# Row maxima of a sparse attention: one product of 128 rows a head, or two heads at once in products of 64 rows

## The chip, the cores and the metric

The kernel runs on one core of a Trainium2 chip. The metric is the time of one execution in microseconds (us) on the device; the median of several executions is compared. TensorE (PE in the rows) multiplies matrices, VectorE (DVE) reduces and adds, ScalarE (ACT) takes exponentials and copies, GpSimd (POOL) adds and masks, and SyncE (SP) issues most DMAs.

## The reference, cut to what matters

One layer of a decoder: a mixer of three kinds of heads, then a feed-forward block, for 1024 tokens of width 1024 in float32. The part that is changed belongs to the sparse attention with 8 query heads of 64 dimensions in two groups of four; each group shares its keys. With 1024 tokens there are 16 blocks of 64 keys, all of which are selected, so the "selected" branch is plain causal attention, and the "window" branch is causal attention over the last 512 keys.

```
s = jnp.einsum('bgrqd,bgqnld->bgrqnl', qblk, ksb)            # selected branch
p = masked_softmax(s, smask)
...
s = jnp.einsum('bgrqd,bgkd->bgrqk', qblk, kwb)               # window branch
o_win = jnp.einsum('bgrqk,bgkd->bgrqd', masked_softmax(s, wmask), vwb)
```

masked_softmax subtracts the largest score of each row before it takes the exponential, and divides by the sum. A number near the largest score serves as well, since it cancels in the division.

## The kernel before, in words

All products of full precision are made of halves: a float32 number is split into a leading half (hi) and a rest (lo) in a short format (fp32r), and hi·hi, lo·hi and hi·lo are added up in PSUM.

Stage by stage: projections and the first two mixers (to about 440 us of the profiled execution), the sparse attention together with the output projection (about 440 to 790 us), the feed-forward block (the rest). In the sparse attention the 1024 queries are swept in 8 blocks of 128, from the last (7) to the first (0). For each block there are two passes over the scores.

- The maxima (`ns_max`, lines L1012 to L1062). For each branch and each head, QS (128 partitions: 64 rows of leading halves of the queries, then 64 rows of rests) is the stationary matrix, and KH (the leading halves of the keys, held twice, in partitions 0 to 63 and 64 to 127) streams past it, up to 512 keys at a time: a product of 128 rows that sums hi·hi and lo·hi (L1037, tiles `nsms` and `nsmw`). A group of nb heads shares a bank of PSUM (one head of 512 or 384 keys, two of 256, four of 128). Where a causal or window edge lies in it, a small bf16 product with the identity adds the mask (L1044). VectorE then takes the negated maximum of each row (L1047, `ns_nm`). When all are done, they are transposed and written by DMA into two rows of M2 (L1061).
- The scores and values (`ns_attn`). The scores are made again with the maxima inside the product (L1077 with M2, L1078 with QS), exponentiated (L1079), and multiplied with the values in products of 64 columns, two at a time (L1097, tiles `nsos`, `nsow`). L1127 sums denominators in products of 32 columns.

The mixer before it has products of 64 rows as well: L513 (tile `mla`) multiplies heads in turn on partitions 0 to 63 and 64 to 127, into two banks, behind products of 32 rows (L510).

The order on each engine is set when the program is built. `merge` interleaves lists of tasks by stated costs: the maxima of the next block beside the scores of the present one, and the output projection (L929, `wo`) as filler. A scheduler then moves single instructions within what data and banks allow. The banks for the maxima (`mx`) are three for block 7 and two for the others: `set_banks(st=(0, 1), ot=(2,), ch=(3,), mt=(7,), rw=(3,), mx=(4, 5), d=(6, 7))`.

`ns_q` loads the queries of a block by three DMAs of 256 KB: hi into QS[0:64], lo into QS[64:128], hi into M2[0:64].

Of the kernel before, what the change touches and what calls it, by code (L numbers as in the profile page):

```python
# [12 lines left out]
ALU = mybir.AluOpType  # L13
AX = mybir.AxisListType
PSUM = bass.MemoryType.PSUM

P = 128
# [14 lines left out]
def f32(ap):  # L32
    return ap.bitcast(F32)
# [3 lines left out]
def kernel(  # L37
# [20 lines left out]
    nc = tc.nc  # L58
# [22 lines left out]
    def unit(name, shape=(P, 1024), dt=F32):  # L81
        v = up.tile([P, UW], dt, tag="u", name=name)[:, 0:math.prod(shape[1:])]
        return v.rearrange("p (a b) -> p a b", a=shape[1]) if len(shape) == 3 else v
# [4 lines left out]
    def bank(name, shape=(P, 512), tag="d"):  # L88
        ids = groups[tag]
        turns[tag] = turns.get(tag, -1) + 1  # L90
        i = ids[turns[tag] % len(ids)]
        return mm.tile(list(shape), F32, tag=f"p{i}", name=name, bufs=1)
# [29 lines left out]
    def small(name, n, dt=F32, p=P, bufs=None):  # L122
        return sm.tile([p, n], dt, tag=name, name=name, bufs=bufs)
# [13 lines left out]
    identb = const.tile([P, P], BF16, name="identb")  # L137
# [191 lines left out]
    def run(tasks):  # L329
        for _, fn in tasks:  # L330
            fn()
# [103 lines left out]
    cols = mlp.tile([P, 3, NT, 4], F32, name="cols", bufs=1)  # L435
# [195 lines left out]
    KH, KL = {}, {}  # L631
# [319 lines left out]
    def ntile(name, shape, tag):  # L951
        pool, bufs = (wkp[0], 3) if tag == "pt" else (wkn, {"acc": 4, "hc": 3, "ot": 2, "y": 3}[tag])
        return pool.tile(shape, F32, tag=tag, name=name, bufs=bufs)
# [3 lines left out]
    CB, CN = "w", 1  # L957
    ns_st = [dict() for _ in range(NT)]

    def ns_q(qt):  # L960
        st = ns_st[qt]
        st["y"] = ntile(f"yns{qt}", [P, 512], "y")
        QS = unit(f"QS{qt}", (P, 8, P), F32R)
        M2 = unit(f"M2{qt}", (P, 8, P), F32R)
        for dst, z in ((QS[0:64], 0), (QS[64:128], 1), (M2[0:64], 0)):
            src = nq_d[z, 0, :, qt * P:(qt + 1) * P]
            nc.sync.dma_start(f32(dst), bass.AP(tensor=src.tensor, offset=src.offset,
                                                ap=[[S, 64], [64 * S, 8], [1, P]]))
        st["QS"], st["M2"] = QS, M2
        st["nm"] = small("ns_nm", 16, bufs=3)  # L970
        st["nm2"] = small("ns_nm2", 16, bufs=3)
        st["cf"] = small("ns_cf", 24, bufs=4)

    def ns_cmp_score(qt, i):
        st = ns_st[qt]
        if i == 0:
            st["c"] = bank(f"nsc{qt}", tag="ch")
            nc.tensor.matmul(st["c"].rearrange("p (h c) -> p h c", h=8), identb,
                             mcmp[:, qt, None, :].to_broadcast([P, 8, 64]), start=True, stop=False)
        h, z = i // 2, i % 2  # L980
        nc.tensor.matmul(st["c"][:, h * 64:(h + 1) * 64], st["QS"][:, h, :], (kcs_h, kcs_l)[z][:, h // 4, :],
                         start=False, stop=(i == 15))

    def ns_cmp(qt):
        st = ns_st[qt]
        gt = gns[:, qt, :].rearrange("p (h b) -> p h b", b=3)
        sps = st["c"]
        nmc = small("nmc", 8)
        nc.vector.tensor_reduce(nmc, sps.rearrange("p (h c) -> p h c", h=8), axis=AX.X, op=ALU.max, negate=True)
        nc.vector.tensor_scalar(nmc, nmc, 1e29, None, op0=ALU.min)  # L990
        pc = ntile(f"pc{qt}", [P, 8, 64], "hc")
        dn = small("nsd", 8, bufs=2)
        for h in range(8):
            nc.scalar.activation(pc[:, h, :], sps[:, h * 64:(h + 1) * 64], AF.Exp, bias=nmc[:, h:h + 1],
                                 accum_out=dn[:, h:h + 1])
        nc.vector.tensor_scalar(dn, dn, 1e-30, None, op0=ALU.max)
        nc.vector.reciprocal(dn, dn)
        nc.vector.tensor_tensor(dn, dn, gt[:, :, 0], op=ALU.mult)
        nc.vector.tensor_tensor(pc, pc, dn[:, :, None].to_broadcast([P, 8, 64]), op=ALU.mult)
        pt = bank(f"nscT{qt}", tag="ch")  # L1000
        for j in range(4):
            nc.tensor.transpose(pt[:, j * P:(j + 1) * P], pc[:, 2 * j:2 * j + 2, :].rearrange("p a c -> p (a c)"), ident)
        pcT = ntile(f"pcT{qt}", [P, 4, P], "hc")
        nc.scalar.copy(pcT.rearrange("p j q -> p (j q)"), pt)
        py = bank(f"nscy{qt}", tag="ch")
        for j in range(4):
            nc.tensor.matmul(py[:, j * P:(j + 1) * P], pcT[:, j, :], vcs[:, j // 2].rearrange("p a d -> p (a d)"),
                             start=True, stop=True)
        nc.scalar.copy(st["y"], py)

    def ns_range(br, qt):
        k0 = 0 if br == "s" else max(0, qt - 4)  # L1012
        return k0, qt + 1 - k0

    def ns_max(qt):
        st = ns_st[qt]
        tasks = []
        cs = [(0.1, lambda i=i: ns_cmp_score(qt, i)) for i in range(16)]
        for bi, br in enumerate(("s", "w")):
            k0, nk = ns_range(br, qt)  # L1020
            kl = nk * P
            for pi, off in enumerate(range(0, kl, 512)):
                w = min(512, kl - off)
                nb = 512 // w

                def piece(h0, bi=bi, br=br, pi=pi, off=off, w=w, nb=nb, k0=k0, kl=kl):
                    hs = range(h0, min(8, h0 + nb))
                    mx_ = bank(f"nsm{br}{qt}_{off}_{h0}", tag="mx")
                    n = len(hs)
                    m3 = mx_[:, 0:n * w].rearrange("p (h k) -> p h k", h=n)  # L1030
                    mk = []
                    if br == "w" and qt >= 4 and off == 0:
                        mk.append((0, mtail))
                    if off + w == kl:
                        mk.append((w - P, mdiag))
                    for i, h in enumerate(hs):
                        nc.tensor.matmul(m3[:, i, :], st["QS"][:, h, :], KH[br, h // 4][:, k0 * P + off:k0 * P + off + w],  # L1037
                                         start=(i == 0), stop=(i == n - 1 and not mk))
                        if br == CB:
                            for _ in range(CN if w >= 256 else 0):  # L1040
                                if cs:
                                    cs.pop(0)[1]()
                    for z, (c0, m) in enumerate(mk):
                        nc.tensor.matmul(m3[:, :, c0:c0 + P], identb, m[:, None, :].to_broadcast([P, n, P]),  # L1044
                                         start=False, stop=(z == len(mk) - 1))
                    dst = (st["nm"] if pi == 0 else st["nm2"])[:, 8 * bi + h0:8 * bi + h0 + n]
                    nc.vector.tensor_reduce(dst, m3, axis=AX.X,  # L1047
                                            op=ALU.max, negate=True)
                    if pi == 1 and h0 + n >= 8:
                        a = st["nm"][:, 8 * bi:8 * bi + 8]  # L1050
                        nc.vector.tensor_tensor(a, a, st["nm2"][:, 8 * bi:8 * bi + 8], op=ALU.min)
                for h0 in range(0, 8, nb):
                    tasks.append((0.42 * w * min(nb, 8) / 1000.0 + 0.05, lambda h0=h0, f=piece: f(h0)))

        def rows():
            pt = bank(f"nsr{qt}", tag="rw")
            nc.tensor.transpose(pt[0:16, 0:P], st["nm"], ident)
            mr = small("ns_mr", P, F32R, 16, bufs=1)
            nc.vector.tensor_copy(mr, pt[0:16, 0:P])
            for bi in range(2):  # L1060
                nc.sync.dma_start(f32(st["M2"][64 + bi:65 + bi, :, :]), f32(mr[8 * bi:8 * bi + 8, :]))  # L1061
        tasks.append((0.15, rows))  # L1062
        return [(0.05, lambda: ns_q(qt))] + tasks + [(CC + 0.05, lambda: (run(cs), ns_cmp(qt)))]

    def ns_attn(qt):
# [83 lines left out]
    T0 = (0,)  # L1149
    set_banks(d=(0,), ch=(0,), mt=(0,), rw=(4,), ds=(2, 3), mx=(4, 5, 1), dt=(6,), po=(7,))  # L1150
    merge((da[-CUT:], 1.0), (wo_loads(0) + merged((ns_max(ORDER[0]), 1.0), (wo_tasks(0, T0), 1.0)), 1.0))
    qstk.close()
    wkp.append(nstk.enter_context(tc.tile_pool(name="wkp", bufs=3, side="right")))
# [197 lines left out]
    w = ff_first  # L1351
    for c in range(NP):
# [5 lines left out]
        if c + 1 < NP:  # L1358
            w = []
# [186 lines left out]
```

## Time and profile before

| | |
|---|---|
| median of 3 runs | 1459.52 us (1459.01 to 1461.6) |
| the profiled execution | 1457.8 us, its span 1456.1 us |
| TensorE busy | 1408.1 us (97% of the span) |
| VectorE, ScalarE, GpSimd busy | 983.0, 661.1, 315.9 us |
| mean granted TensorE clock | 0.991 |

The span goes from the first to the last instruction of the profiled execution. [...]

### The profile page before, as it was taken

The page shows a single profiled execution, that of the slowest core. Times are in us where ns is not written, and L with a number is a line of the kernel's source. Part 1 is how long each engine was busy: PE and PEld are TensorE (multiplying, and loading weights), DVE is VectorE, ACT ScalarE, POOL GpSimd, SP SyncE. Part 2 cuts the span into 40 slices and gives each one's busy share as a digit, 9 for nine tenths or more (in the row PEclk, how much of TensorE's full clock was granted, in tenths as well). Part 3 has the DMA queues.
Part 4 walks back from the last instruction along what each step waited for, and adds up shares of the span by engine and source line. Part 5 has one row for each costly group of instructions (what it writes and reads, how often), then busy time and mean ns, then how long its engine had stood idle before and what let it go on. Part 6 is the DMA issues. An engine that isn't in the chain of part 4 may idle for free.

```text
span 1456.1 us, 19441 instructions
## 1 busy us (share of the span) xinstructions
PE 1408.1 (97%) x7031; PEld 1066.8 (73%) x7031; DVE 983.0 (68%) x1756; ACT 661.1 (45%) x1309; POOL 315.9 (22%) x358
## 2 busy tenths in 40 slices
PE   8999999899989999999999999999999999999997
PEld 7998777666756555556666887888888788788875
DVE  6313588788778665766545968777776877985366
ACT  6414333687572433334444545555544543443243
POOL 2000033222241343443333111111111004200051
PEclk9999999999988999999999999999999999999999
DMA  6301222111255011012312327444435896796522
GB/s 214 102 1 30 69 89 93 52 33 37 80 133 121 30 37 44 15 37 73 95 52 73 109 87 233 154 147 139 146 137 214 294 407 216 278 357 191 174 88 115
DMA packets 107551, 181.77 MB, mean 125 GB/s; under 512 B 11552, under 2 KB 66368, under 8 KB 107456
## 3 DMA queue, kind: packets, MB, share of 16 engines
q1 hardware_dynamic: 96704, 144.89, 31.1%
q0 software_dynamic: 10752, 35.66, 6.4%
q8 instruction: 55, 0.90, 0.3%
q14 instruction: 40, 0.33, 0.1%
HBM read 134.31 MB, written 46.14 MB: 124 GB/s over the span
## 4 chain that ended last, share of the span: by engine, by line
PE 78%; DVE 9%; ACT 4%; issue 3%; POOL 2%; DMA 2%; DVEq 0%; SPq 0%; POOLq 0%; ACTq 0%
PE ff L1417 17%; PE ff L1320 15%; PE wo L929 6%; PE ff L1252 4%; PE pml_p L324 3%; PE nsos L1097 2%; PE nq_p L324 2%; PE pD_p L244 2%; PE pB_p L244 2%; PE dao L871 2%; PE pC_p L244 2%; PE nsow L1097 2%; PE pA_p L244 1%; POOL x2b L1435 1%; PE nsms L1037 1%
## 5 line engine op out<-in xcount | busy, mean ns | idle before, releaser
L1320 PE MATMUL ff<-h2h,fw 128*128 128x512 f32 x312 | 97.5, 393 | 1.0 <-ACT fw L126 0.7
L1226 POOL DMA_DIRECT2D act_d<-fn x52 | 28.1, 540 | 206.2 <-ACT fn L1334 151.6
L1320 PEld LDWEIGHTS ff<-h2h,fw 128*128 128x128 f32 x312 | 58.6, 188 | 15.0 <-ACT fw L126 1.2
L1079 ACT ACTIVATE nsps<-nsts 128x512 f32<-128x512 f32 x72 | 40.1, 596 | 64.1 <-PE nsts L1078 44.7
L1327 DVE TENSOR_TENSOR fn<-fn,ff 128x512 f32<-128x512 f32 x65 | 43.5, 686 | 35.9 <-PE ff L1320 35.9
L835 DVE TENSOR_REDUCE da_nm<-das 128x1 f32<-128x512 f32 (+3 forms) x96 | 51.5, 551 | 18.6 <-PE das L832 16.0
L126 ACT ACTIVATE fw<-fs 128x512 fp32r<-128x512 f32 x52 | 32.6, 632 | 66.5 <-PE ff L1320 65.1
L1320 PE MATMUL ff<-h2l,fw 128*128 128x512 f32 x156 | 61.1, 392 | 0.0
L1047 DVE TENSOR_REDUCE ns_nm<-nsms 128x1 f32<-128x512 f32 (+3 forms) x76 | 48.5, 656 | 18.5 <-PE nsms L1044 9.2
L841 ACT ACTIVATE dap<-das,da_nm 128x512 f32<-128x512 f32 (+3 forms) x96 | 55.1, 584 | 12.7 <-DVE da_nm L838 6.8
L1435 POOL TENSOR_TENSOR x2b<-x2b,tmq 128x512 f32<-128x512 f32 x12 | 22.0, 1871 | 152.6 <-ACT tmq L1454 152.6
L1417 PE MATMUL ff<-b0h,a0h 128*128 128x512 f32 x128 | 50.4, 395 | 2.5 <-ACT fn L1333 2.5
L1079 ACT ACTIVATE nspw<-nstw 128x512 f32<-128x512 f32 x60 | 33.3, 604 | 39.1 <-PE nstw L1078 26.4
L1417 PE MATMUL ff<-b1l,a1h 128*128 128x512 f32 x128 | 50.5, 394 | 0.5 <-DVE b1l L128 0.5
L1417 PE MATMUL ff<-b0h,a0l 128*128 128x512 f32 x128 | 50.6, 395 | 0.0
L1417 PE MATMUL ff<-b2h,a2l 128*128 128x512 f32 x128 | 50.4, 394 | 0.0
L1417 PE MATMUL ff<-b1h,a1h 128*128 128x512 f32 x128 | 50.3, 393 | 0.0
L1417 PE MATMUL ff<-b1h,a1l 128*128 128x512 f32 x128 | 50.3, 393 | 0.0
L1417 PE MATMUL ff<-b2h,a2h 128*128 128x512 f32 x128 | 50.3, 393 | 0.0
L1417 PE MATMUL ff<-b2l,a2h 128*128 128x512 f32 x128 | 50.2, 392 | 0.0
L1417 PE MATMUL ff<-b0l,a0h 128*128 128x512 f32 x128 | 50.1, 392 | 0.0
L931 DVE TENSOR_TENSOR x<-x,wo 128x512 f32<-128x512 f32 x32 | 22.0, 686 | 40.2 <-PE wo L929 40.2
(548 smaller groups left out, 4313.2 us busy)
## 6 DMA issues: line engine op xcount, KB each, us to landing
ar<-act_d SPq DMA_DIRECT2D x48, 512.0 KB
f1r<-in_w_ff_dram SPq DMA_DIRECT2D x32, 512.0 KB
wr<-in_w_ff_dram SPq DMA_DIRECT2D x32, 512.0 KB
act_d<-fn POOLq DMA_DIRECT2D x52, 256.0 KB, 2.6
x<-in_x_dram SPq DMA_DIRECT2D x16, 512.0 KB
act_d<-as POOLq DMA_DIRECT2D x16, 512.0 KB, 3.3
wo<-in_w_ff_dram SPq DMA_DIRECT2D x16, 512.0 KB
wr<-in_w_ff_dram SPq DMA_DIRECT2D x32, 256.0 KB
```

The lines of the kernel that those rows point to most:

```text
L244: nc.tensor.matmul(pt[:, :NA], T_stat(a, kt, t), b[kt // 4][:, kt % 4, :], start=(i == 0), stop=(i == 23))
L324: nc.tensor.matmul(pt, a[:, kt, :], T_mov(b, kt, h), start=(i == 0), stop=(i == 23))
L835: nc.vector.tensor_reduce(nm[:, z:z + 1], b[:, 0:n1 - n0], axis=AX.X, op=ALU.max, negate=True)
L841: nc.scalar.activation(p_[:, n0:n1], b[:, 0:n1 - n0], AF.Exp, bias=nm[:, 0:1], accum_out=dens[:, 2 * z + m:2 * z + m + 1])
L929: nc.tensor.matmul(po, m_[a][:, k, :], wo[4 * part + k][b][:, ns_], start=(i == 0), stop=(i == 11))
L1047: nc.vector.tensor_reduce(dst, m3, axis=AX.X, op=ALU.max, negate=True)
L1079: nc.scalar.activation(pT[:, g, :], s_, AF.Exp)
L1097: nc.tensor.matmul(st["o", br][64 * g:64 * g + 64, :], vsw[kt // 4][:, kt % 4, c0:c0 + 64], pT[:, g, :], start=(k == 0), stop=(k == nk - 1))
L1252: nc.tensor.matmul(pt, a, T_mov(b, kt, h), start=(i == 0), stop=(i == 23))
L1320: nc.tensor.matmul(pt, w[:, x_, kt, :], b[y_][kt // 2][:, kt % 2, :], start=(i == 0), stop=(i == 11))
L1327: nc.vector.tensor_tensor(dst, s_, pt, op=ALU.add)
L1417: nc.tensor.matmul(banks[4 * p + t], a[y][:, 512 * p + t * P:512 * p + t * P + P], b[x_][:, 512 * p:512 * p + 512], start=first and i == 0 ...
```

## The change

The row maxima are taken of hi·hi alone; lo·hi is left out of them (the scores themselves are made as before). A product of a head then needs 64 rows. Two heads, or two groups of nb heads, form a pair: one on partitions 0 to 63 (QS[0:64] with KH[0:64]) into one bank, the other on partitions 64 to 127 (M2[64:128], into which a fourth DMA now loads the hi queries, with KH[64:128]) into the next bank. The mask products of both banks stand behind the pair's products, and the two reductions behind these.

```
-        for dst, z in ((QS[0:64], 0), (QS[64:128], 1), (M2[0:64], 0)):
+        for dst, z in ((QS[0:64], 0), (QS[64:128], 1), (M2[64:128], 0), (M2[0:64], 0)):
...
-                    mx_ = bank(f"nsm{br}{qt}_{off}_{h0}", tag="mx")
-                    m3 = mx_[:, 0:n * w].rearrange("p (h k) -> p h k", h=n)
...
-                    for i, h in enumerate(hs):
-                        nc.tensor.matmul(m3[:, i, :], st["QS"][:, h, :], KH[br, h // 4][:, k0 * P + off:k0 * P + off + w],
-                                         start=(i == 0), stop=(i == n - 1 and not mk))
+                    mx_ = [bank(f"nsm{br}{qt}_{off}_{h}", tag="mx")[:, 0:n * w].rearrange("p (h k) -> p h k", h=n)
+                           for h in (h0, h0 + n)]
+                    for i in range(n):
+                        for u, (rs, T) in enumerate(((slice(0, 64), "QS"), (slice(64, 128), "M2"))):
+                            h = h0 + n * u + i
+                            nc.tensor.matmul(mx_[u][:, i, :], st[T][rs, h, :], KH[br, h // 4][rs, cols],
+                                             start=(i == 0), stop=(i == n - 1 and not mk))
                         if br == CB:
-                            for _ in range(CN if w >= 256 else 0):
+                            for _ in range(2 * CN if w >= 256 else 0):
                                 if cs:
                                     cs.pop(0)[1]()
-                    for z, (c0, m) in enumerate(mk):
-                        nc.tensor.matmul(m3[:, :, c0:c0 + P], identb, m[:, None, :].to_broadcast([P, n, P]),
-                                         start=False, stop=(z == len(mk) - 1))
-                    dst = (st["nm"] if pi == 0 else st["nm2"])[:, 8 * bi + h0:8 * bi + h0 + n]
-                    nc.vector.tensor_reduce(dst, m3, axis=AX.X,
-                                            op=ALU.max, negate=True)
+                    for u in range(2):
+                        for z, (c0, m) in enumerate(mk):
+                            nc.tensor.matmul(mx_[u][:, :, c0:c0 + P], identb, m[:, None, :].to_broadcast([P, n, P]),
+                                             start=False, stop=(z == len(mk) - 1))
+                    for u in range(2):
+                        h = h0 + n * u
+                        dst = (st["nm"] if pi == 0 else st["nm2"])[:, 8 * bi + h:8 * bi + h + n]
+                        nc.vector.tensor_reduce(dst, mx_[u], axis=AX.X, op=ALU.max, negate=True)
...
-                for h0 in range(0, 8, nb):
-                    tasks.append((0.42 * w * min(nb, 8) / 1000.0 + 0.05, lambda h0=h0, f=piece: f(h0)))
+                for h0 in range(0, 8, 2 * nb):
+                    tasks.append((0.84 * w * nb / 1000.0 + 0.1, lambda h0=h0, f=piece: f(h0)))
```

The scheduler makes a new order of this. On TensorE, at the window maxima of block 7 (heads 2, 3, 4; `nsmw_0_2` is head 2, `mtail` the mask of the window's edge), there stood before:

```order
L1037 MATMUL nsmw_0_2_4875<-KHw_4404,QS_4648 128x512
L1044 LDWEIGHTS identb
L1044 MATMUL nsmw_0_2_4875<-mtail,identb 128x128
L1037 MATMUL nsmw_0_3_4880<-KHw_4404,QS_4648 128x512
L1044 LDWEIGHTS identb
L1044 MATMUL nsmw_0_3_4880<-mtail,identb 128x128
```

and now, where QS is the lower and M the upper half of the rows:

```order
L871 MATMUL dao_7_4832<-daPT_7_0_1_4845,dav_930 64x128
L1040 MATMUL nsmw_0_2_4876<-KHw_4404,QS_4648 128x512
L1040 MATMUL nsmw_0_3_4877<-KHw_4404,M_4649 128x512
L1048 LDWEIGHTS identb
L1048 MATMUL nsmw_0_2_4876<-mtail,identb 128x128
L1048 LDWEIGHTS identb
L1048 MATMUL nsmw_0_3_4877<-mtail,identb 128x128
L863 MATMUL daT_7_4_0_4906<-ident,dap_7_4620 128x128 x3
```

Here the two heads of a pair stand side by side, and so do their masks. At the first maxima of block 6, on the same engine, there stood before:

```order
L1037 MATMUL nsms_0_3_5044<-KHs_4204,QS_5015 128x512
L1037 MATMUL nsms_0_0_5023<-KHs_4204,QS_5015 128x512
L1037 MATMUL nsms_0_5_5065<-KHs_4207,QS_5015 128x512
L929 MATMUL wo_1_0_5223<-woh_4578,mTh_1_5219 128x512
L1037 MATMUL nsms_0_2_5038<-KHs_4204,QS_5015 128x512
L1037 MATMUL nsms_0_7_5080<-KHs_4207,QS_5015 128x512
```

and now:

```order
L1040 MATMUL nsms_0_1_5026<-KHs_4204,M_5017 128x512
L916 MATMUL mT_1_5221<-ident,mix_1_5219 128x128
L1062 MATMUL nsr_4943<-ident,ns_nm 16x128
L916 MATMUL mT_1_5221<-ident,mix_1_5219 128x128 x3
L1040 MATMUL nsms_0_0_5025<-KHs_4204,QS_5016 128x512
L929 MATMUL wo_1_0_5230<-woh_4578,mTh_1_5226 128x512
L1040 MATMUL nsms_0_3_5041<-KHs_4204,M_5017 128x512
L1002 MATMUL nscT_4974<-ident,pc_4960 128x128 x4
L1040 MATMUL nsms_0_2_5040<-KHs_4204,QS_5016 128x512
```

Here the scheduler has set products of 128 rows between the heads of a pair, since the second head's bank comes free later than the first's.

## Rows read from the trace of the kernel before

**Rows 1.** The page's first row: busy time of each engine, its share, instructions

```profile
PE 1408.1 (97%) x7031; PEld 1066.8 (73%) x7031; DVE 983.0 (68%) x1756; ACT 661.1 (45%) x1309; POOL 315.9 (22%) x358
```

**Rows 2.** Busy time of each engine by stretch, then granted clock, DMA share, GB/s

```profile
443.00:467.00 24.00, 23.40 (x159) 16.55 (x158) 21.75 (x43) 4.11 (x10) 2.18 (x4) 1.00 0.44 98
467.00:500.00 33.00, 29.78 (x105) 14.95 (x107) 25.54 (x45) 16.78 (x53) 11.20 (x10) 0.84 0.20 58
500.00:755.00 255.00, 250.07 (x1241) 153.10 (x1239) 155.91 (x245) 100.16 (x237) 97.88 (x76) 1.00 0.16 49
```

**Rows 3.** TensorE's waits from 435 to 760 us: us in total, times, longest

```profile
PE nsms L1037 <- DVE ns_nm L1047: 3.1, 4, 1.7
...
PE nsmw L1037 <- DVE ns_nm L1047: 0.4, 1, 0.4
```

**Rows 4.** Groups by line and shape: count, busy us, mean ns, idle before

```profile
L1037 PE MATMUL nsms<-KHs,QS 128*128 128x512 f32 x48 | 21.5, 490 | 1.7 <-DVE ns_nm L1047 1.5
L1037 PE MATMUL nsmw<-KHw,QS 128*128 128x512 f32 x40 | 17.8, 453 | 0.4 <-DVE ns_nm L1047 0.4
...
L1047 DVE TENSOR_REDUCE ns_nm<-nsms 128x1 f32<-128x512 f32 x48 | 32.1, 684 | 10.9 <-PE nsms L1037 8.8 <-PE nsms L1044 1.8
```

**Rows 5.** TensorE in order of time: start, length, line, rows*columns, x count

```profile
247.84 0.39 PE L324 MATMUL nq_p<-hTl,nq_hi 128*128 128x512 f32 x1
248.16 0.49 PE L510 MATMUL mla<-cmD,selr 32*128 32x256 f32 x2
248.58 0.71 PE L513 MATMUL mla<-mlqk,mlqk 64*128 64x128 f32 x8
249.23 0.50 PE L324 MATMUL daq_p<-hTh,daq_hi 128*128 128x512 f32 x1
249.56 0.39 PE L324 MATMUL daq_p<-hTh,daq_lo 128*128 128x512 f32 x1
249.79 0.39 PE L324 MATMUL daq_p<-hTl,daq_hi 128*128 128x512 f32 x1
```

**Rows 6.** The same view of 248.57 to 248.60 us alone

```profile
248.58 0.38 PE L513 MATMUL mla<-mlqk,mlqk 64*128 64x128 f32 x2
```

**Rows 7.** The same view around a visit of products of 64 columns

```profile
662.67 0.39 PE L1078 MATMUL nstw<-QS,KHw 128*128 128x512 f32 x1
662.99 1.08 PE L1097 MATMUL nsow<-nspw,vsw 128*64 128x512 f32 x4
664.00 0.50 PE L1077 MATMUL nstw<-M,KLw 66*128 66x512 f32 x1
664.33 0.40 PE L1078 MATMUL nstw<-QS,KHw 128*128 128x512 f32 x1
```

**Rows 8.** The same view: products of 64 and of 256 columns streamed

```profile
451.92 0.28 PE L981 MATMUL nsc<-kcs_h,QS 128*128 128x64 f32 x1
452.03 0.28 PE L981 MATMUL nsc<-kcs_l,QS 128*128 128x64 f32 x1
...
534.87 0.40 PE L1037 MATMUL nsms<-KHs,QS 128*128 128x256 f32 x2
535.11 0.28 PE L1044 MATMUL nsms<-mdiag,identb 128*128 128x256 bf16 x1
```

**Rows 9.** The same view: heads with a mask, and two masks in a row

```profile
490.28 0.28 PE L1044 MATMUL nsms<-mdiag,identb 128*128 128x128 bf16 x2
490.50 1.08 PE L1097 MATMUL nsos<-nsps,vsw 128*64 128x512 f32 x4
...
622.89 0.47 PE L1037 MATMUL nsms<-KHs,QS 128*128 128x512 f32 x1
623.21 0.23 PE L1044 MATMUL nsms<-mdiag,identb 128*128 128x128 bf16 x1
623.25 0.48 PE L1037 MATMUL nsms<-KHs,QS 128*128 128x512 f32 x1
```

**Rows 10.** The DMA queue's issues that write M2 from the stored queries

```profile
M<-nq_d SPq DMA_DIRECT2D x8, 256.0 KB
```

More of the change, by code (lines that the diff above doesn't have):

```diff
@@ L1026, in piece @@
                 def piece(h0, bi=bi, br=br, pi=pi, off=off, w=w, nb=nb, k0=k0, kl=kl):
-                    hs = range(h0, min(8, h0 + nb))
-                    mx_ = bank(f"nsm{br}{qt}_{off}_{h0}", tag="mx")
-                    n = len(hs)
-                    m3 = mx_[:, 0:n * w].rearrange("p (h k) -> p h k", h=n)
+                    n = nb
+                    cols = slice(k0 * P + off, k0 * P + off + w)
                     mk = []
@@ L1046, in piece @@
-                    dst = (st["nm"] if pi == 0 else st["nm2"])[:, 8 * bi + h0:8 * bi + h0 + n]
-                    nc.vector.tensor_reduce(dst, m3, axis=AX.X,
-                                            op=ALU.max, negate=True)
-                    if pi == 1 and h0 + n >= 8:
+                    for u in range(2):
+                        for z, (c0, m) in enumerate(mk):
+                            nc.tensor.matmul(mx_[u][:, :, c0:c0 + P], identb, m[:, None, :].to_broadcast([P, n, P]),
+                                             start=False, stop=(z == len(mk) - 1))
@@ L1050, in piece @@
+                    for u in range(2):
+                        h = h0 + n * u
+                        dst = (st["nm"] if pi == 0 else st["nm2"])[:, 8 * bi + h:8 * bi + h + n]
+                        nc.vector.tensor_reduce(dst, mx_[u], axis=AX.X, op=ALU.max, negate=True)
+                    if pi == 1 and h0 + 2 * n >= 8:
                         a = st["nm"][:, 8 * bi:8 * bi + 8]
                         nc.vector.tensor_tensor(a, a, st["nm2"][:, 8 * bi:8 * bi + 8], op=ALU.min)
-                for h0 in range(0, 8, nb):
-                    tasks.append((0.42 * w * min(nb, 8) / 1000.0 + 0.05, lambda h0=h0, f=piece: f(h0)))
+                for h0 in range(0, 8, 2 * nb):
+                    tasks.append((0.84 * w * nb / 1000.0 + 0.1, lambda h0=h0, f=piece: f(h0)))
```

## The prediction, made before the changed kernel ran

> **What bounds the kernel now.** The page's first row: TensorE is busy 97% of the span, no other engine over 68% [rows 1]. Averages mix stages, so next the busy time by stretch, over the time in which the maxima are made: TensorE is busy 23.4 of 24, 29.8 of 33 and 250.1 of 255 us, VectorE 155.9 of the last 255 [rows 2]. From 443 to 755 us TensorE therefore sets the pace, with 312 − 303.25 = 8.8 us of idle time. Third, what it waits for there: for the products of the maxima 3.5 us in all, each time for VectorE's reduction to free a bank [rows 3]. So a microsecond that TensorE saves or loses there counts almost fully, and what VectorE does counts only through banks.
>
> Fourth, what a product costs. Its record of 0.39 us is not its price: in order of time, products of 512 columns start 0.23 us apart [rows 5]. Those of 256 take 0.24 / 2 = 0.12, and those of 64 or 128 columns 0.11, where the load of the weights sets the pace [rows 8]; for 384 I scale 0.23 to 0.17.
>
> **What is removed: the second head of a pair.** There are 192 head products: 88 of 512 columns [rows 4], 24 of 384, 24 of 256 and 56 of 128, counted in the order. Two heads side by side on different halves of the rows should cost one: in the mixer before, the products of 64 rows do so, since two start within 0.03 us of each other [rows 6]. That row shows it for 128 columns; for 512 no row does.
>
> But a pair saves only where its heads stand side by side. In the order of the changed kernel that holds for 23 pairs of 512, 6 of 384, 8 of 256 and 24 of 128; 42 of the 88 heads of 512, about half, stand alone. The saving: 23 × 0.23 + 6 × 0.17 + 8 × 0.12 + 24 × 0.11 = 5.3 + 1.0 + 1.0 + 2.6 = **9.9 us**.
>
> **What is added: steps in and out of products of 64 rows.** The view in order of time shows what a visit to another shape of the array costs. From 247.84 to 249.56 us TensorE goes from full products to 32 rows, to 64 rows and back, in 1.72 us [rows 5]. Plain prices for the same work: 0.23 + 2 × 0.12 + 4 pairs × 0.11 + 0.23 = 1.14. The 0.58 over that falls on three steps, **0.19 us a step**. One half of it shows as the late start of the next product (0.32 for 0.23 going in), the other as a slow first product (0.33 for 0.23 coming out). The visit to 64 columns has the same two signs, 0.32 and 0.33 [rows 7]: after a step the weights are not loaded behind the product that runs, but in the open. Beside a narrow product, where the load sets the pace anyway, I charge only one half, 0.10; that is an estimate from these two rows.
>
> The order has 96 visits to 64 rows. Into them: 31 from wide products (0.19 each, 5.9 us), 36 from narrow ones or masks (0.10, 3.6 us), and 29 straight from a visit to 64 or 32 columns, where the step out of that was paid before (0). Out of them: 13 to wide products (2.5 us), 23 to narrow ones (2.3), 3 to column visits (0.3), and 57 to a mask. The last cost nothing new: a full product followed by a bf16 mask already starts the mask 0.32 after itself instead of 0.23 [rows 9]. Sum **+14.6 us** for 106 paid steps, 0.14 on average.
>
> **What is moved: the masks.** Their number stays (105, now 106), but in the order they stand in 70 groups where there were 104. A head with its mask takes 0.36 us, 0.13 over a bare one [rows 9]. The second of two masks still has to run. Where two stand in a row, the visit to 64 columns behind them starts 0.22 after the first; less the 0.09 of a late start that is 0.06 a mask [rows 9]. So each group less saves 0.07, with 0.13 as the upper bound (the second mask free) and 0.05 as the lower: 34 × 0.07 = **−2.4 us**.
>
> **What is only covered.** VectorE makes the same reductions at 0.68 us [rows 4], off the path that sets the end. SP issues 8 more loads of 256 KB, a fourth beside three for each block [rows 10], ahead of M2's lower half and of the loads for the output projection behind it on the queue. The DMA engines are at 0.16 to 0.44 there [rows 2], and the order issues the loads of a block before the scores of the block before it, so I cost them at nothing; without that cover the upper head, and the scores and `wo` products queued behind it on TensorE, wait for one more load a block. The pair now wants both banks of `mx`. The scheduler has answered with the separated heads, which is charged above; what it leaves of waiting I set equal to the 3.5 us of now, with nothing and twice that as bounds.
>
> **The sum.** +14.6 − 9.9 − 2.4 = **+2.3 us**. On the profiled execution that is 1457.8 + 2.3 = 1460.1; the median of the runs lies 1.7 above that execution, so 1459.5 + 2.3 = **1461.8 us**. A measurement of this kernel can tell about 0.2%, which is 2.9 us.
>
> The row on two products of 64 rows shows that a pair costs one head while TensorE stays in that shape [rows 6], and the row on the visit that getting there costs 0.19 a step [rows 5]. The Trainium skill, TensorEngine Tiling (Array Packing), section Theoretical Speedup, puts the factor at up to 2 for a contraction of 64 or less; its section Key Properties warns that a change of tiling mode drains TensorE. By the factor alone the sum would be the −16.7 us that stands under "all of it" below; by the rows it is the +2.3 above. The trace agrees with the warning.
>
> **The rivals.**
>
> *Dearer: the pairs do not overlap at 512 columns, or every step costs the full 0.19.* For it: rows 6 are of 128 columns, where the load of the weights hides what two streams into two banks do. Against it: nothing in the trace. No saving on the 23 wide pairs makes +2.3 + 5.3 = +7.6 us; all 106 steps at 0.19 make 20.1 − 9.9 − 2.4 = +7.8. Either gives about **1467**, both 1473.
>
> *New waits.* A pair needs two free banks and one more load; behind the waiting product stand the scores that ScalarE needs. If the waits of rows 3 double and a block's start slips by 0.2 us eight times, it is +2.3 + 3.5 + 1.6 = +7.4 at worst, **1465** in the middle. Against it: VectorE has 35% of its time free.
>
> *Faster: cheap steps.* Here the change ends on the other side. If every one of the 106 steps costs only the late start, 0.10, they make 10.6, and with 0.13 for each mask group saved (4.4) the sum is −3.7: **1455.8**. It decides at a mean of 0.12 a step. For it: many steps lie beside other steps or masks, where both halves may merge. Against it: the 0.58 of rows 5 lies beside such steps too, and is not merged. The idle time of 467 to 500 us, where the clock stands at 0.84 [rows 2], could also shrink by the new order, by a similar 3 to 4 us.
>
> *All of it.* Every pair overlaps and no step costs anything: half of 88 × 0.23 + 24 × 0.17 + 24 × 0.12 + 56 × 0.11 = 33.4, so −16.7 us, **1442.8**. The order speaks against it, as half of the wide heads stand alone.
>
> **How the numbers follow.** Nearly balanced, within 2.9 us: 0.40. Dearer 0.20 and new waits 0.15, both slower: 0.35. Cheap steps or a luckier order 0.22 and all of it 0.03, both faster: 0.25. The predicted time is the balanced 1461.8. The range goes up over the single dearer cases, not to both at once, and down past the cheap steps, 1455 to 1469; it leaves out "all of it" and the ends of the dearer cases, not quite 2 in 10. The likeliest case's own range is 1456.6 to 1462.4.
>
> **What would show it.** In the changed trace, order of time: a pair of 512 columns starts within 0.03 us and the next product 0.4 us later (overlap right) or 0.6 (wrong). A full product before a lone head starts it 0.32 later, and the one after the head is slow by 0.1: steps right. TensorE's busy time between 443 and 760 us up by about 2.3 us, with the stage as much longer. Waits of the head products for `ns_nm` near 3.5 us, none for the loads of M2. Wrong would be: a stage shorter by over 3 us (steps cheaper than charged), or longer by over 5 with pairs that start one after the other (no overlap), or with idle time on `ns_nm` (banks). Any difference after 800 us, where the feed-forward block runs as before, would not be from this sum.

## The result and the profile after

| kernel | median of its runs | ratio to before, 95% interval |
|---|---|---|
| before | 1459.3 us (6 runs, 1457.8 to 1462.8) | |
| changed | 1476.7 us (6 runs, 1470.3 to 1495.6) | 1.0120 [1.0086, 1.0154] |

The change makes the kernel 1.2% slower: 17.4 us by the medians, 15.4 by the two profiled executions (spans 1471.5 and 1456.1 us). That is beyond the predicted range of 1455 to 1469. The changed kernel also scatters more, and its time goes with the granted clock: 1470.3 us at a mean of 0.983, 1478.0 at 0.976, 1492.0 at 0.967. (The longest run, and the profiled run of experiment 4 below, are slow ones, over 1.5% above the fastest of the same kernel: the ratios leave them out, and no trace of them is read here.)

First the page's row of busy time, beside [rows 1]:

```profile
PE 1431.6 (97%) x7031; PEld 1068.7 (73%) x7031; DVE 983.2 (67%) x1756; ACT 661.0 (45%) x1309; POOL 318.1 (22%) x358
```

TensorE still sets the pace, and is busy 23.5 us longer with as many instructions. Next the busy time by stretch, as in [rows 2] (PE, PEld, DVE, ACT, POOL, granted clock, DMA share, GB/s):

```profile
443.00:467.00 24.00, 23.43 (x99) 15.13 (x100) 16.39 (x33) 2.69 (x7) 2.18 (x4) 0.78 0.58 110
467.00:500.00 33.00, 32.71 (x130) 19.01 (x127) 18.03 (x34) 12.30 (x46) 5.93 (x7) 0.66 0.32 84
500.00:755.00 255.00, 252.62 (x1202) 139.06 (x1201) 159.46 (x252) 103.23 (x241) 97.39 (x75) 1.00 0.18 49
```

The last stretch keeps its clock of 1.00. In the first two the granted clock is 0.78 and 0.66, where it was 1.00 and 0.84, and in the first TensorE gets through 99 products where it made 159. Third, slices of 5 us inside these, of the changed kernel:

```profile
455.00:460.00 5.00, 5.00 (x27) 3.15 (x25) 3.24 (x5) 0.00 (x0) 0.00 (x0) 0.99 0.05 11
460.00:465.00 5.00, 5.00 (x24) 3.29 (x23) 3.51 (x9) 0.43 (x1) 0.72 (x1) 0.69 0.00 0
465.00:470.00 5.00, 5.00 (x27) 3.38 (x26) 1.39 (x3) 0.16 (x1) 1.46 (x3) 0.50 0.06 16
470.00:475.00 5.00, 5.00 (x18) 2.91 (x17) 2.66 (x4) 0.87 (x2) 0.00 (x0) 0.50 0.00 0
```

TensorE is recorded busy without a gap, before the clock falls and after, and yet it goes to 0.50, the lower of its two levels, 1.2 GHz. So it isn't idle time that came in. The view of its waits says the same, beside the 3.5 us of [rows 3]:

```profile
PE nsms L1040 <- DVE ns_nm L1053: 0.8, 3, 0.3
...
PE nsmw L1040 <- DVE ns_nm L1053: 0.3, 1, 0.3
```

Waits for banks fell from 3.5 to 1.1 us. Last, how long the stage is. For each kernel, the view of the heads' products (duration in ns as least, median and most; then the first and the last start) gives the time from the first head of the selected branch to the last of the window branch; before, then changed:

```profile
L1037 PE MATMUL nsms<-KHs,QS x96: 221/397/796, 443.8 to 738.6; 128*128 128x512 f32 x48, 128*128 128x384 f32 x16, 128*128 128x256 f32 x16, 128*128 128x128 f32 x16
L1037 PE MATMUL nsmw<-KHw,QS x96: 221/352/505, 456.9 to 742.9; 128*128 128x512 f32 x40, 128*128 128x128 f32 x40, 128*128 128x384 f32 x8, 128*128 128x256 f32 x8
```

```profile
L1040 PE MATMUL nsms<-KHs,QS x48: 269/440/792, 445.2 to 752.7; 64*128 64x512 f32 x24, 64*128 64x384 f32 x8, 64*128 64x256 f32 x8, 64*128 64x128 f32 x8
...
L1040 PE MATMUL nsmw<-KHw,M x48: 268/435/793, 465.0 to 758.1; 64*128 64x512 f32 x20, 64*128 64x128 f32 x20, 64*128 64x384 f32 x4, 64*128 64x256 f32 x4
```

From 443.8 to 742.9 is 299.1 us, from 445.2 to 758.1 is 312.9: the stage of the maxima is 13.8 us longer. It begins 1.4 us later, and 0.2 of the 15.4 are left for all that follows.

### The profile page after: what moved, and what is told of

It is laid out like the page before. It is cut to its first block, busy times and chain, and to the rows that moved or that the text cites. A ratio compares the mean times of both kernels' runs of the same rounds, so it can differ in the third digit from the quotient of the medians.

```text
span 1471.5 us, 19461 instructions
## 1 busy us (share of the span) xinstructions
PE 1431.6 (97%) x7031; PEld 1068.7 (73%) x7031; DVE 983.2 (67%) x1756; ACT 661.0 (45%) x1309; POOL 318.1 (22%) x358
## 4 chain that ended last, share of the span: by engine, by line
PE 82%; DVE 8%; ACT 3%; POOL 2%; issue 2%; DMA 2%; DVEq 0%; POOLq 0%; SPq 0%; ACTq 0%
PE ff L1422 17%; PE ff L1325 16%; PE wo L929 6%; PE ff L1257 4%; PE pml_p L324 3%; PE nq_p L324 2%; PE nsos L1102 2%; PE dao L871 2%; PE pD_p L244 2%; PE pB_p L244 2%; PE pC_p L244 2%; PE nsms L1040 2%; PE nsow L1102 2%; PE nsmw L1040 1%; PE pA_p L244 1%
## 5 line engine op out<-in xcount | busy, mean ns | idle before, releaser
L1053 DVE TENSOR_REDUCE ns_nm<-nsmw 128x1 f32<-128x512 f32 (+3 forms) x62 | 39.4, 667 | 22.5 <-PE nsmw L1048 22.1
```

The source lines that it names most:

```text
L1053: nc.vector.tensor_reduce(dst, mx_[u], axis=AX.X, op=ALU.max, negate=True)
```

## The experiments

Two measures serve for all of them. **Stage** is the time just read, from the first to the last head product. **Time at the lower level** is worked out from the granted clock c of 447 to 515 us, in which blocks 7 and 6 have their maxima: 68 us × 2 × (1 − c). The rows of before and of the changed kernel, in this order:

```profile
447.00:515.00 68.00, 64.20 (x310) 38.42 (x309) 52.12 (x94) 23.45 (x66) 18.54 (x19) 0.92 0.19 47
```

```profile
447.00:515.00 68.00, 67.04 (x267) 38.09 (x265) 44.44 (x84) 22.24 (x65) 15.11 (x16) 0.77 0.29 69
```

That is 10.9 us for before and 31.3 for the changed kernel. Three theories stood against each other: the clock (A), waits and the new order (B), and the price of the steps between shapes (C). All experiments compare medians of 4 to 12 runs with runs of the kernel before on the same chip: one chip for 1 to 4, one for 5 to 8, one for 9, where before takes 1460.9, 1460.0 and 1460.0 us. (The 29 us at half clock that two expectations give for before are of its whole execution.)

**1. The new order with products of 128 rows.** Order, banks, grouped masks and the fourth load of the changed kernel stay; each head takes all of QS and KH, so lo·hi is in the maxima again.

```
-    nc.tensor.matmul(mx_[u][:, i, :], st[T][rs, h, :], KH[br, h // 4][rs, cols], ...
+    nc.tensor.matmul(mx_[u][:, i, :], st["QS"][:, h, :], KH[br, h // 4][:, cols], ...
```

> The changed kernel with the same pairs, banks, loads and the same order of instructions, but each head's product again has all 128 rows (QS with the whole of KH), so no step to another shape of the array is left. It computes hi.hi + lo.hi as before the change. Theory A (the clock: the visits to 64 rows let the granted clock fall to 1.2 GHz between 460 and 490 us): time at half clock back near the 29 us of before, time 1457 to 1462. Theory B (order, banks, fourth load: new waits): it keeps the loss, 1470 to 1476. Theory C (direct price of the steps, no clock): 1457 to 1462 too, and the clock of the changed kernel would have been an accident.

Measured: 1450.5 us, ratio 0.9930 [0.9918, 0.9942], the fastest kernel of this study, and 6.5 us under the least that any theory expected. On TensorE its order is that of the changed kernel but for a few products ahead of the first maxima. Its windows of blocks 7 and 6:

```profile
447.00:515.00 68.00, 65.89 (x348) 40.03 (x347) 56.24 (x102) 27.47 (x74) 20.41 (x20) 1.00 0.28 68
...
470.00:475.00 5.00, 3.86 (x18) 2.44 (x19) 5.00 (x17) 2.02 (x8) 2.34 (x4) 1.00 0.06 14
```

No time at the lower level, though TensorE sits idle for 1.14 of the 5 us from 470 on. And the view of its heads' products:

```profile
L1040 PE MATMUL nsms<-KHs,QS x96: 274/394/584, 446.4 to 732.1; 128*128 128x512 f32 x48, 128*128 128x384 f32 x16, 128*128 128x256 f32 x16, 128*128 128x128 f32 x16
L1040 PE MATMUL nsmw<-KHw,QS x96: 229/337/505, 459.5 to 737.1; 128*128 128x512 f32 x40, 128*128 128x128 f32 x40, 128*128 128x384 f32 x8, 128*128 128x256 f32 x8
```

The stage is 290.7 us, 8.4 under before. So the order and the load cost nothing, they gain, and B falls. The 64-row shape alone costs 312.9 − 290.7 = 22.2 us.

**2. Products of 66 rows in the order of before.** 66 rows are taken to be no smaller shape of the array (L1077 has them too, [rows 7]; the lag below bears it out), so there are no steps and no pairs; of lo·hi two rows of 64 stay in the maxima.

```
-    nc.tensor.matmul(m3[:, i, :], st["QS"][:, h, :], KH[br, h // 4][:, ...], ...
+    nc.tensor.matmul(m3[:, i, :], st["QS"][0:66, h, :], KH[br, h // 4][0:66, ...], ...
```

> The kernel before, with one edit: each head's product takes the first 66 of the 128 rows (all leading halves, two rows of the rests; the remaining 62 rows of the rests are left out of the maxima). 66 rows need no step to another shape. Theory A1 (half the rows in use is what lets the clock fall): more time at half clock than the 29 us of before in 440 to 500 us, 1463 to 1473. Theory A2 (the steps in and out are what lets it fall): as before, 1457 to 1462. Theories B and C: as before, 1457 to 1462.

Measured: 1471.9 us, ratio 1.0074 [1.0060, 1.0087]. Nothing but the rows in use was changed, and TensorE gets the same products in the same order as before. The windows:

```profile
447.00:515.00 68.00, 65.03 (x259) 38.86 (x259) 47.28 (x85) 21.56 (x62) 16.04 (x17) 0.72 0.18 45
...
455.00:460.00 5.00, 5.00 (x29) 3.90 (x29) 4.29 (x11) 0.00 (x1) 0.51 (x1) 0.72 0.02 3
460.00:465.00 5.00, 5.00 (x25) 3.36 (x26) 1.14 (x2) 0.58 (x1) 1.68 (x4) 0.50 0.16 25
```

The clock is down here too with TensorE busy all the time. The heads' products:

```profile
L1037 PE MATMUL nsms<-KHs,QS x96: 225/402/797, 444.4 to 750.0; 66*128 66x512 f32 x48, 66*128 66x384 f32 x16, 66*128 66x256 f32 x16, 66*128 66x128 f32 x16
L1037 PE MATMUL nsmw<-KHw,QS x96: 222/396/796, 457.7 to 754.2; 66*128 66x512 f32 x40, 66*128 66x128 f32 x40, 66*128 66x384 f32 x8, 66*128 66x256 f32 x8
```

38.1 us at the lower level, 27.2 more than before, and a stage of 309.8 us, 10.7 longer. As the order is the same, one product can be sought in both traces. The head at 500.54 us of before is the one at 511.69 here:

```profile
500.54 0.50 PE L1037 MATMUL nsmw<-KHw,QS 128*128 128x512 f32 x1
```

```profile
511.69 0.55 PE L1037 MATMUL nsmw<-KHw,QS 66*128 66x512 f32 x1
```

The lag is 0.6 us at the first head, 11.15 here, where the last time at the lower level ends, and 11.3 at the last head, 242 us later. So the whole loss falls into the time in which the clocks differ, and at a clock of 1.00 66 rows cost what 128 do. A is confirmed without any step. It also gives a rate: 10.7 / 27.2 = 0.39 us lost for each us at 1.2 GHz (an estimate, from rounded clocks).

**3 and 4. The change in blocks 5 to 0 alone, and in blocks 7 and 6 alone.** Each has the pairs and masks of the changed kernel in its blocks, and the code of before in the others (`if qt <= 5`, `if qt > 5`); the fourth load stands in all blocks of both.

> The change in blocks 5 to 0 alone; blocks 7 and 6 have the products of 128 rows. Theory A: the stretch up to 500 us keeps its clock, and what is left is the direct price of the steps in the other blocks, 0 to +3 us: 1458 to 1464. Theory B: waits come with every block, about three quarters of the loss: 1468 to 1472. Theory C: three quarters of the loss as well, 1468 to 1472.

> The change in blocks 7 and 6 alone; the others have the products of 128 rows. Theory A: nearly the whole loss, with 55 to 70 us at half clock, 1468 to 1476. Theory B and theory C: a quarter of the loss, 1462 to 1465.

Measured: 1458.1 us, ratio 0.9982 [0.9972, 0.9992], for blocks 5 to 0; 1479.8 us, ratio 1.0123 [1.0106, 1.0139], for blocks 7 and 6, more than the 1468 to 1476 expected. The loss of the changed kernel comes with blocks 7 and 6, where its clock falls. But the 0.2% for blocks 5 to 0 is no gain of these blocks. In that kernel blocks 7 and 6 have the products of before, with the fourth load and in another order, and there the clock holds:

```profile
447.00:515.00 68.00, 65.26 (x343) 39.53 (x341) 56.02 (x101) 26.95 (x73) 20.24 (x20) 1.00 0.32 71
```

Here are two products up to which it and the kernel before have done the same work on TensorE; of before, then of the kernel with the change in blocks 5 to 0:

```profile
503.36 0.39 PE L929 MATMUL wo<-wol,mTh 128*128 128x512 f32 x1
...
717.62 1.08 PE L1097 MATMUL nsos<-nsps,vsw 128*64 128x512 f32 x4
```

```profile
498.76 0.39 PE L929 MATMUL wo<-wol,mTh 128*128 128x512 f32 x1
...
718.42 1.08 PE L1133 MATMUL nsos<-nsps,vsw 128*64 128x512 f32 x4
```

(L1133 is L1097 of before.) It is 4.6 us ahead at the first and 0.8 behind at the second. So the change costs about 5 us in the later blocks, at a clock of 1.00. The first two gain some 6 without it, as the first head started 1.9 us later than before (445.7 for 443.8).

**5. The kernel of experiment 1 without the fourth load.**

```
-        for dst, z in ((QS[0:64], 0), (QS[64:128], 1), (M2[64:128], 0), (M2[0:64], 0)):
+        for dst, z in ((QS[0:64], 0), (QS[64:128], 1), (M2[0:64], 0)):
```

> The order of the changed kernel (two heads to a task, masks of both behind them) with products of 128 rows, and without the fourth load of a block. Two banks and one load more were the price that the theory of new waits named. If the load cost something, this ends below the 1450.5 us of the same kernel with the load, by 1 us or more; if it is hidden, as the prediction held, it ends at 1450.5 within 2 us. Granted clock 1.00 between 467 and 755 us either way.

Measured: 1454.9 us, ratio 0.9957 [0.9941, 0.9973]. Less work, and 4.4 us slower, which neither theory expected. Without the load the scheduler makes another order in blocks 7 and 6, and the lower level comes back for a few us:

```profile
447.00:515.00 68.00, 65.08 (x336) 39.79 (x334) 56.25 (x102) 25.40 (x70) 19.13 (x19) 0.97 0.20 54
```

In 68 × 2 × 0.03 = 4.1 us at the lower level, at the rate of experiment 2 about 1.6 us are lost, and the stage, from 448.1 to 740.9 us, is 2.1 longer than in experiment 1. The rest of the 4.4 falls outside the stage and is not explained. That the load itself is hidden is not contradicted, but not shown by itself either.

**6. 64 rows in blocks 5 to 0, 128 rows in blocks 7 and 6, in the order of experiment 1.** This prices the steps and the pairs at a clock of 1.00. The edit, against experiment 1:

```
+    R = slice(0, P) if qt >= 6 else rs
-    nc.tensor.matmul(mx_[u][:, i, :], st["QS"][:, h, :], KH[br, h // 4][:, cols], ...
+    nc.tensor.matmul(mx_[u][:, i, :], st[T if qt < 6 else "QS"][R, h, :], KH[br, h // 4][R, cols], ...
```

> As the kernel with 128 rows in the new order (1450.5 us), but the maxima of blocks 5 to 0 in products of 64 rows, and only those. The prediction's own prices for these six blocks: 68 paid steps +9.2, 45 pairs -7.5, so +1.8 us; with 0.10 for each of the 27 exits into a mask, which it charged at nothing, +4.5. Theory that the clock carries most of the loss: the clock stays at 1.00 in 500 to 755 us, and the time is 1452 to 1455. Theory that each step costs far more than charged (the 22.8 us of the changed kernel over the one with 128 rows, spread over all 96 visits): two thirds of it, about 1465.

Measured: 1456.9 us, ratio 0.9977 [0.9966, 0.9989]; 6.4 us over experiment 1 by the medians, which is above the range expected of the theory of the clock and far from the 1465 of dear steps. The window of blocks 7 and 6:

```profile
447.00:515.00 68.00, 65.86 (x342) 39.69 (x342) 53.98 (x97) 27.26 (x73) 21.04 (x21) 1.00 0.28 66
```

The clock holds. The first and the last group of the heads' products:

```profile
L1041 PE MATMUL nsms<-KHs,QS x64: 270/440/580, 444.0 to 734.4; 128*128 128x512 f32 x24, 64*128 64x512 f32 x12, 128*128 128x384 f32 x8, 64*128 64x256 f32 x8
...
L1041 PE MATMUL nsmw<-KHw,M x32: 270/410/502, 532.5 to 739.8; 64*128 64x512 f32 x12, 64*128 64x128 f32 x12, 64*128 64x384 f32 x4, 64*128 64x256 f32 x4
```

The stage is 295.8 us, 5.1 longer than in experiment 1. The prediction's prices give +1.8; with 0.10 for the 27 exits into a mask, +4.5. The rest of the shape's 22.2 us, 17.1, is lost by blocks 7 and 6.

**7. 128 rows, of which 64 hold zeros.** In about the order of experiment 5, and like it without the fourth load, the maxima are made of M2, whose lower half holds the leading halves and whose upper half GpSimd has set to zero. The maxima have the same numbers as in the changed kernel.

```
+        nc.gpsimd.memset(f32(M2[64:128]), 0.0)
...
+    nc.tensor.matmul(mx_[u][:, i, :], st["M2"][:, h, :], KH[br, h // 4][:, cols], ...
```

> Products of 128 rows in about the order of the lean kernel, whose second 64 rows of the stationary matrix are zeros (M2[0:64] holds the leading halves, M2[64:128] is set to zero by GpSimd ahead of the maxima): the same maxima as the changed kernel computes. If the clock follows the rows that the instruction names, it stays as with 128 rows and the time is that of the lean kernel, about 1450. If it follows the rows that hold anything, 443 to 500 us falls to the lower clock as in the kernel with 66 rows, and the time is 8 to 16 us longer, 1458 to 1466.

Measured: 1456.5 us, ratio 0.9977 [0.9965, 0.9989], 1.6 us over experiment 5, the lean kernel that the expectation took to be at 1450. The window of blocks 7 and 6:

```profile
447.00:515.00 68.00, 64.23 (x330) 39.24 (x329) 56.41 (x101) 25.51 (x70) 19.16 (x21) 0.97 0.21 48
```

The same 0.97 as there. So in this pair of kernels the clock goes by the rows that the instruction names, not by what stands in them.

**8. 64 rows, every head alone, in the order of before.** As experiment 2 with 64 for 66, so beside that one it adds the steps (and lo·hi is left out of the maxima).

> The kernel before in its own order, with QS[0:64] and KH[0:64] alone in the maxima (lo.hi left out): every head stands alone, in 64 rows in place of the 66 of the second experiment, so beside that one (1471.9 us) it only adds the steps in and out. By the prediction's prices 142 paid steps are +18.8 us, 1490.7; with 0.10 for each of 75 exits into a mask +26.3, 1498.2. If steps cost nothing: 1472.

Measured: 1499.5 us, ratio 1.0263 [1.0244, 1.0282]. The window of blocks 7 and 6:

```profile
447.00:515.00 68.00, 66.72 (x234) 37.24 (x234) 40.26 (x77) 17.97 (x57) 9.61 (x12) 0.65 0.27 63
```

And the heads' products:

```profile
L1037 PE MATMUL nsms<-KHs,QS x96: 270/439/793, 447.8 to 780.5; 64*128 64x512 f32 x48, 64*128 64x384 f32 x16, 64*128 64x256 f32 x16, 64*128 64x128 f32 x16
L1037 PE MATMUL nsmw<-KHw,QS x96: 269/436/792, 464.7 to 785.1; 64*128 64x512 f32 x40, 64*128 64x128 f32 x40, 64*128 64x384 f32 x8, 64*128 64x256 f32 x8
```

27.6 us over experiment 2 by the medians, 27.5 by the stage (337.3 us). At 47.6 us the lower level lasts 9.5 us longer than there, at the rate of 0.39 that is 3.7; 23.8 are left for the steps, between the 18.8 that the prediction's prices give and the 26.3 with 0.10 for every exit into a mask. So steps do cost what the rows said, and a little more.

**9. Two heads to a task, the rest as before.**

```
-                for h0 in range(0, 8, nb):
-                    tasks.append((0.42 * w * min(nb, 8) / 1000.0 + 0.05, lambda h0=h0, f=piece: f(h0)))
+                for h0 in range(0, 8, 2 * nb):
+                    tasks.append((0.84 * w * nb / 1000.0 + 0.1,
+                                  lambda h0=h0, f=piece, nb=nb: (f(h0), f(h0 + nb))))
```

> The kernel before, with two heads (or two groups of heads) to a task as in the changed kernel, but each head with its own bank, its products of 128 rows, and its mask right behind them as before; no fourth load. It tells where the gain of the new order (1450.5 with the load, 1454.9 without, against 1460) is from. If it is from the masks in a row (68 to 70 groups in place of 105), this ends at the time of before, 1460 within 2 us. If it is from the coarser tasks alone, it ends at 1453 to 1456.

Measured: 1456.5 us, ratio 0.9979 [0.9965, 0.9993]. It lies between the two expectations, 0.5 above the upper end of the second and 1.5 below the lower end of the first. Part of the new order's gain is from the coarser tasks alone; how much the masks in a row add can't be told, as this interval overlaps that of experiment 5.

## Why the prediction was wrong

**The step that failed is the price list, in "what a product costs" and in "the sum": every product was charged at the price of a clock of 1.00, as if the change could not move the clock.** The trace of before [rows 2] showed 0.84 in 467 to 500 us, so the clock already fell in this stage at times, but the prediction used that row only as a chance to gain. Experiment 2 shows the fall with rows alone, 3 that blocks 5 to 0 keep the clock with 64 rows, 4 that the loss comes with blocks 7 and 6, and 7 that 128 rows hold the clock as well if half are zeros. Why blocks 5 to 0 keep it is only argued: there the maxima are thinned out by scores, values and output projection, while in blocks 7 and 6 they stand close together.

The stage's 13.8 us come apart so, term by term:

| term | predicted | by the runs |
|---|---|---|
| clock: (31.3 − 10.9) × 0.39 | 0 | +8.0 |
| pairs and steps: 22.2 of experiment 1, less 31.3 × 0.39 = 12.2 | +4.7 | +10.0 |
| masks in groups, new order: −8.4 of experiment 1, plus 10.9 × 0.39 = 4.2 of clock | −2.4 | −4.2 |
| sum | +2.3 | +13.8 |

The column ends at 13.8 because its terms are made of stages that differ by that; what the runs give is the split, and it hangs on the 0.39. The changed kernel's own runs give another figure: that of 1492.0 us has 48 us more at the lower level than that of 1470.3 (clocks 0.967 and 0.983 over spans of 1490.2 and 1468.5 us) and takes 21.7 us more, 0.45 each (an estimate, as the other). With that the clock is 9.2 and the pairs and steps 8.1. A third reading needs no rate, as the changed kernel and experiment 1 have one order from 448 us on. A mask and a `wo` product, of experiment 1, then of the changed kernel:

```profile
459.10 0.23 PE L1048 MATMUL nsms<-mdiag,identb 128*128 128x128 bf16 x1
...
475.93 0.40 PE L929 MATMUL wo<-woh,mTl 128*128 128x512 f32 x1
```

```profile
461.73 0.23 PE L1048 MATMUL nsms<-mdiag,identb 128*128 128x128 bf16 x1
...
489.82 0.50 PE L929 MATMUL wo<-woh,mTl 128*128 128x512 f32 x1
```

Between them the changed kernel's clock is at its lower level, and its lag grows from 2.6 to 13.9 us: 11.3 of the 22.2, the steps in these 28 us included. At 0.39 the 27.2 us from 461.9 to 489.1, all at the lower level, make 10.6 of that.

**Overlap: right.** In order of time, in the changed kernel:

```profile
489.39 0.50 PE L1040 MATMUL nsms<-KHs,QS 64*128 64x512 f32 x1
489.39 0.49 PE L1040 MATMUL nsms<-KHs,M 64*128 64x512 f32 x1
489.82 0.50 PE L929 MATMUL wo<-woh,mTl 128*128 128x512 f32 x1
490.15 0.40 PE L929 MATMUL wo<-wol,mTh 128*128 128x512 f32 x1
490.39 0.40 PE L929 MATMUL wo<-woh,mTh 128*128 128x512 f32 x1
490.72 0.50 PE L1040 MATMUL nsms<-KHs,QS 64*128 64x512 f32 x1
491.14 0.50 PE L929 MATMUL wo<-woh,mTl 128*128 128x512 f32 x1
491.48 0.39 PE L929 MATMUL wo<-wol,mTh 128*128 128x512 f32 x1
491.71 0.40 PE L1082 MATMUL nsts<-M,KLs 66*128 66x512 f32 x1
```

Two heads of 512 columns start together and the next product 0.43 us later, as a lone head's next product does (0.42). So it is all along at a clock of 1.00: behind 17 pairs of 512 columns the next product of another shape starts after 0.42 to 0.45 us, behind 26 lone heads after 0.42 or 0.43. A pair does cost one head.

**Steps at wide products: right.** From 490.39 to 491.71 four products take 1.32 us; four at 0.23 are 0.92. The 0.40 over is the step in and the step out, 0.20 each where 0.19 was charged. The start of the head is late by 0.10 and the rest shows behind it, as [rows 5] had it.

**Exits into a mask: charged at nothing, cost about 0.1 each.** The lone head with a mask:

```profile
458.28 0.28 PE L981 MATMUL nsc<-kcs_h,QS 128*128 128x64 f32 x1
458.49 0.49 PE L1040 MATMUL nsms<-KHs,QS 64*128 64x512 f32 x1
458.91 0.23 PE L1048 MATMUL nsms<-mdiag,identb 128*128 128x128 bf16 x1
```

The mask starts 0.42 after the head, where a full product had it at 0.32 [rows 9]: a late mask and a step add up, they don't merge; 13 of the 26 lone heads have a mask behind them, and it always starts after 0.42 or 0.43. Solved for this one price, the pairs and steps of the changed kernel give (10.0 − 4.7) / 57 = 0.09, experiment 6 (5.1 − 1.8) / 27 = 0.12, and experiment 8 (23.8 − 18.8) / 75 = 0.07. At 0.09 it is 5.3 us for the 57 exits, the second largest miss.

**Masks and order: right sign, too small.** Of the −4.2 the runs don't tell the masks from the coarser tasks (experiment 9), nor from the order that the fourth load brings (experiments 3 and 5).

**Banks and waits: right, and better than charged** (1.1 us for 3.5). **After 800 us: right**, no difference worth the name. The rival "dearer" came nearest in its sign but not in its cause: steps dearer than charged alone would have ended at about 1465 us (1461.8 + 5.3 for the exits − 1.8 for the masks and the order), inside the range. What took the time out of it was the clock.

## What to carry to other kernels

Halving the rows of a product is not free even where TensorE stays the only limit: count, before the saving, whether the stretch keeps its clock, and look for granted clocks under 1.00 there already. By the prices found, work in a smaller shape pays only in long visits in which both halves run side by side (no run here has such visits alone); here about half of the wide heads stood alone, and a visit between full products cost 0.4 us, more than the 0.23 that the second head of a pair saves. The gain in this case lay in the order that came with the change: with full products it is 0.7% faster than before and needs no smaller shape.

## What the runs showed of the hardware

The granted clock went to 1.2 GHz with TensorE recorded busy for 5.00 of 5 us, when the maxima used 64 or 66 rows, and stayed at 2.4 GHz through a slice with 3.86 of 5 us busy, when they used 128. The Trainium skill, TensorE: Matmul & The Clock Gate, section "What's actually happening", says that the clock is set by how busy the engine has been of late, and its section "HAM oscillation" tells of falls behind waits for DMA. No such wait stands ahead of the changed kernel's fall, as TensorE is recorded busy for all of 455 to 465 us. Recorded busy time did not foretell the clock here: with the same products in the same order (experiments 1 and 2) it went by the rows that the maxima name, and 64 rows of zeros did as well as full ones (experiment 7).

A us at the lower level cost 0.39 us here by experiment 2, and 0.45 by the changed kernel's own runs. And less work can be slower by way of the order: the kernel with one load of 256 KB less per block took 4.4 us more (on another chip; the ratios to before are 0.9957 and 0.9930).
